# Two transformer blocks on one core: a block inversion that starts from blocks of 16, and a planner that offers other work more often

## The chip, the cores and the metric

The kernel runs on one core of a Trainium2 chip. The metric is the device time of one execution in microseconds; the number given for a kernel is the median of its runs. The profile is one further execution, recorded by the hardware profiler. Its engines are called PE (TensorE's matrix products; PEld is its loading of weights), DVE (VectorE), ACT (ScalarE), POOL (GpSimd) and SP (SyncE, which here only issues DMAs).

## What is computed

The reference chains two networks on a sequence of 512 tokens of width 1024. The first has two layers (windowed attention, neighbourhood attention, memory attention, feed-forward parts). The second is one layer with two branches beside each other, an RWKV-7 time mix and a convolution, and then a feed-forward part. The change is in the two branches:

```python
def step(S, inp):                       # RWKV-7, per head, token by token
    r_t, w_t, k_t, v_t, a_t, b_t = inp
    sa = jnp.einsum('bhvk,bhk->bhv', S, a_t)
    S = S * w_t[:, :, None, :] + sa[..., None] * b_t[:, :, None, :] + v_t[..., None] * k_t[:, :, None, :]
    y = jnp.einsum('bhvk,bhk->bhv', S, r_t)
...
c = u * jax.nn.sigmoid(gate)            # convolution branch: 31 taps per channel, then layer norm and silu
c = lax.conv_general_dilated(c, dw...) + dw_b
c = jax.nn.silu(layer_norm(c, ln_w, ln_b))
```

There are 16 heads of width 64. The kernel doesn't step through tokens: it cuts the 512 tokens into 8 chunks of 64, and within a chunk it has to invert, for each head, a 64x64 triangular matrix with ones on its diagonal.

## The kernel before, in words

**Where the change lies.** The change touches the mixing stage of the second block, some 700 us of the execution, which `drive` (line 1768) emits. Its large products are the input projections, the gates and the two output maps: units of 24 products of 128x128 by 128x512 in three passes (high by high, high by low, low by high), done by `dense` (line 1064). The units stand in a fixed list (lines 1684 to 1689): c0 to c7 are the convolution's two inputs, i0 to i7 the inputs of a pair of heads, g0 to g15 the gates, w0 to w7 the map of the RWKV branch, m0 to m7 the map of the convolution branch. A unit's weights are loaded by SP two units ahead into two buffers ("raw"), split by ACT into a high part (wh) and, in turns by DVE and by POOL, into a low part (wl).

**The streams.** Beside the units run seven generators, the streams: `outs` prepare a pair of heads (`pair_out`, with the gram matrices X and RA), `solves` invert the triangular matrices of a group of two pairs (`solve`, line 1314), `chains` carry the state S through the 8 chunks of a group (`chain`, line 1439), `posts` normalise and gate its result (`post`, line 1480), `mapped_rows` prepare the map's operand, and `ends` does the layer norm of the convolution branch. There are four groups, g = 0 to 3, and for each a solve, a chain and a post, in that order. w0 and w1 do a part of their products and then hold until the fourth post is done; the m units wait for the layer norm.

**How the order is set.** PE's and DVE's instructions stand in the order in which the program emits them. That order is set by a planner (class `Clock`, line 88), which estimates each instruction's cost (`cost`, line 122) and keeps a time for each engine. `dense` yields after each second product of its first two passes, and after some of its last. At each yield `burst` (line 1771) steps those streams whose results the planner takes to be ready: at a full burst all of them, at a minor one only those that last yielded neither BURST nor FREE, so mostly those that have no products next. Line 1078 makes every yield whose count is a multiple of 8 full and the others minor; a unit's last yield is full too.

**The taps.** The convolution's 31 taps for 8 blocks of channels (`conv`, line 1525; acc is the sum) are 240 DVE instructions, dealt out by the class `Taps` (line 199). `until(t)` emits taps while the planner's DVE time plus 0.75 is at most t. It is called after each burst with PE's planned time less 1 us (lines 1792 and 1812), and by the planner ahead of every other DVE instruction, up to the time when that one's operands are ready.

**The solve.** The diagonal 32x32 blocks of each triangular matrix are inverted first. Before the change: the 8x8 diagonal blocks travel through DRAM into the tile x, in a layout with one small matrix per partition, twice 64 partitions; DVE inverts them by seven steps of a product and a sum (lines 1364 to 1367); they travel back and are read as 32x32 blocks (dd), which DVE transposes (dt). Then two doublings follow on PE, 8 to 16 and 16 to 32. Each is made of three `quad`s: 64 products of 32x32 on four tiles of PE beside each other (the trace counts each as two, in two passes), the first of a doubling with the identity added by one product of 512 columns. ACT copies each result out. The first doubling takes the tile e as its operand, which ACT fills from the matrices with a mask. After that come the step from 32 to 64 and the application to the other operands.

Of the kernel before, what the change touches and what calls it, by code (L numbers as in the profile page):

```python
# [16 lines left out]
AF = mybir.ActivationFunctionType  # L17
ALU = mybir.AluOpType
# [4 lines left out]
P = 128  # L23
# [64 lines left out]
class Clock:  # L88
# [33 lines left out]
    def cost(self, engine, op, out, ins):  # L122
        n = max(math.prod(x.shape[1:]) for x in [out, *ins])
        if op == "dma_start":
            n, wide = math.prod(out.shape), len(out.shape) > 2 and out.shape[-1] < P
            return 0.65 if engine == "POOL" else 0.4 if not wide else 0.8 if n == 8192 else 0.65
        if engine == "DVE":
            return (0.21 if op == "scalar_tensor_tensor" else 0.14) + n * (0.00215 if op.endswith("scan") else 0.00107)
        if engine == "ACT":
            return 0.17 + n * 0.00086  # L130
        if op == "memset":
            return 0.1 + n * 0.0008
        return 2.0 if n == 8 else 0.35 + n * 0.0019
# [83 lines left out]
def tile_two_blocks(ctx: ExitStack, tc: tile.TileContext, A, out):  # L217
# [782 lines left out]
    with ExitStack() as es:  # L1000
# [63 lines left out]
        def dense(hl, xh=lambda k: hT_h[:, k, :], xl=lambda k: hT_l[:, k, :], ks=range(KD), ps=None):  # L1064

            h, l = hl
            ps = pst() if ps is None else ps
            n = 0
            for part in range(2):
                for k in ks:  # L1070
                    if part:
                        nc.tensor.matmul(ps, lhsT=l[:, k, :], rhs=xh(k), start=False, stop=k == KD - 1)
                    else:
                        nc.tensor.matmul(ps, lhsT=h[:, k, :], rhs=xh(k), start=k == 0, stop=False)
                        nc.tensor.matmul(ps, lhsT=h[:, k, :], rhs=xl(k), start=False, stop=False)
                    n += 2 - part
                    if n % 2 == 0 and (n < 3 * len(ks) or len(ks) < KD):
                        yield n % 8 != 0
            return ps


# [232 lines left out]
        def solve(g, G):  # L1314
# [4 lines left out]
            def q32(i):  # L1319
                return slice(32 * i, 32 * i + 32)  # L1320

            def d8(t, r):

                return bass.AP(t.tensor, t.offset + 264 * r, [[1024, 64], [32, 8], [1, 8]])

            def quad(lhsT, rhs, eye=False):

                ps = pst("po")
                if eye:
                    nc.tensor.matmul(ps, lhsT=ident, rhs=i32[:, None, :].to_broadcast([P, 16, 32]), start=True, stop=False)  # L1330
                for c in range(16):
                    for i in range(4):
                        nc.tensor.matmul(ps[q32(i), q32(c)], lhsT=lhsT(i)[:, c, :], rhs=rhs(i)[:, c, :],
                                         start=not eye, stop=c == 15 or not eye, tile_position=(32 * i, 32 * i))
                return ps.rearrange("p (q t) -> p q t", t=32)

            def s2(n):
                return el.tile([P, 16, 32], F32, tag="s2", name=n, bufs=3)

            def of(t):  # L1340
                return lambda i: t[q32(i)]
# [1 line left out]
            diag = [ABf[q32(i), :, q32(i % 2)] for i in range(4)]  # L1343

            x = s2("x").rearrange("p q t -> p (q t)")
            at, tt = (x[:, 128 * i : 128 * i + 128].rearrange("p (m a b) -> p m a b", m=2, a=8) for i in range(2))
            pr = x[:, 256:]
            nc.gpsimd.memset(tt, 0.0)
            nc.gpsimd.memset(tt.rearrange("p m a b -> p m (a b)")[:, :, ::9], 1.0)
            yield from there(ab)  # L1350
            for r in range(4):
                nc.sync.dma_start(at[64 * (r // 2) : 64 * (r // 2) + 64, r % 2], d8(ab, r))

            e = s2("e")
            nc.gpsimd.memset(e, 0.0)
            for i in range(4):
                for m in range(2):
                    cols = slice(16 * m + 8, 16 * m + 16)
                    nc.scalar.activation(e[q32(i), :, cols], diag[i][:, :, cols], AF.Copy,
                                         scale=blk[q32(i), P + 33 + m : P + 34 + m])  # L1360
                nc.gpsimd.memset(diag[i][:, :, 0:16], 0.0)
                nc.scalar.activation(diag[i][:, :, 16:], diag[i][:, :, 16:], AF.Copy, scale=blk[q32(i), P : P + 1])
            yield from there(at)
            for t in range(1, 8):
                p4 = pr[:, : 2 * t * t].rearrange("p (m j s) -> p m j s", m=2, s=t)
                nc.vector.tensor_tensor(p4, tt[:, :, :t, :t], at[:, :, None, :t, t].to_broadcast([P, 2, t, t]), ALU.mult)
                nc.vector.tensor_reduce(tt[:, :, :t, t], p4, AX.X, ALU.add)
            yield from there(tt)
            for r in range(4):
                nc.sync.dma_start(d8(td, r), tt[64 * (r // 2) : 64 * (r // 2) + 64, r % 2])  # L1370
            yield from there(td)
            dd, dt = s2("dd"), s2("dt")
            for i in range(4):
# [2 lines left out]
            nc.vector.transpose(dt, dd)  # L1376
            yield BURST

            de = s2("de")
            nc.scalar.activation(de, quad(of(e), of(dt), True), AF.Copy)  # L1380
            yield BURST
            dd_, dt = s2("dd"), s2("dt")
            nc.scalar.activation(dt, quad(of(dd), of(de)), AF.Copy)
            yield FREE
            nc.scalar.activation(dd_, quad(of(de), of(dd)), AF.Copy)
            dd = dd_
            yield BURST
            de = s2("de")
            nc.scalar.activation(de, quad(lambda i: diag[i], of(dt), True), AF.Copy)
            yield BURST  # L1390
# [377 lines left out]
        def drive():  # L1768
# [20 lines left out]
            def stand():  # L1789
                t = clock.free("PE")  # L1790
                clock.t["PE"] = min([s[1] for s in streams if s[1] > t] + [t + 0.5])
                taps.until(clock.t["PE"] - 1)
                burst()

            raws = [u[0]() for u in units[:2]]
# [1 line left out]
            for i, (_, _, run, pre, *_) in enumerate(units):  # L1797
                t = clock.free("PE")
                while pre is not None and not pre():
                    stand()  # L1800
                idle += clock.free("PE") - t
                if i + 2 < len(units):
                    raws.append(units[i + 2][0]())
                nxt, more = None, i + 1 < len(units)
                for n, at_ in enumerate(run(hl) if run is not None else ()):
                    if at_ == HOLD:
                        while posts_done < 4:
                            stand()
                    if more and (at_ == SPLIT or (n == 3 and not units[i][4:])):
                        nxt, more = units[i + 1][1](raws.pop(0)), False  # L1810
                    burst(at_ is True)
                    taps.until(clock.free("PE") - 1)
                if more:
                    nxt = units[i + 1][1](raws.pop(0))
                hl = nxt
# [52 lines left out]
```

## Time and profile before

| | |
|---|---|
| median of 3 runs | 2426.93 us (2425.42 to 2431.42) |
| the profiled execution | 2429.3 us, span 2427.5 us from its first to its last instruction |
| mean granted TensorE clock | 0.969 of full speed |
| PE busy | 2313.3 us, 95% of the span |
| DVE busy | 1198.5 us, 49% |
| ACT busy | 965.3 us, 40% |
| POOL busy | 339.0 us, 14% |

How to read it: 1.8 us of the execution lie outside the span. Busy times of PE overlap a little, because products are pipelined. A low granted clock makes the same product take longer. Line numbers of most rows are those of two helpers (L152 and L192 for what the planner places, L186 for the rest), so rows are told apart by their tiles.

### The profile page before, as it was taken

The numbers are of one execution on the slowest core, as the hardware profiler recorded it, in microseconds if no ns is written. First come the engines' busy times: TensorE is split into PE (matmuls) and PEld (weight loads), VectorE is DVE, ScalarE is ACT, GpSimd is POOL, SyncE is SP. The second block draws the span as 40 slices with busy tenths as digits, with TensorE's granted clock in tenths as the row PEclk, the third lists the DMA queues.
The fourth block names the chain that finished last, engine by engine and source line by source line (L and its number), as shares of the span: only waits on it lengthen the run. The fifth ranks groups of instructions, "written<-read, shape, count | busy, mean of one in ns | idle before, by whom it ended". The sixth has DMA issues, their size and how long they took to land. (4 is left out here: it accounts for less than half of the span.)

```text
span 2427.5 us, 38347 instructions
## 1 busy us (share of the span) xinstructions
PE 2313.3 (95%) x15723; PEld 1862.5 (77%) x15723; DVE 1198.5 (49%) x1832; ACT 965.3 (40%) x1743; POOL 339.0 (14%) x457
## 2 busy tenths in 40 slices
PE   7899999999999999999999889999998699999998
PEld 6756788888798788888887677777776577888886
DVE  4366533234523653223355767778786655422232
ACT  4355423123434543222334645456633523322221
POOL 1000120000200000000012332354333221000000
PEclk9889999999999999999999899999999799999999
DMA  7330673224453144333232232234244254433331
GB/s 205 100 88 18 173 223 109 78 86 131 130 148 105 61 129 123 99 96 96 87 98 88 82 82 76 62 110 112 76 114 156 83 156 165 139 96 96 97 100 55
DMA packets 326543, 262.60 MB, mean 108 GB/s; under 512 B 47152, under 2 KB 294004, under 8 KB 325984
## 3 DMA queue, kind: packets, MB, share of 16 engines
q1 hardware_dynamic: 308552, 211.18, 29.9%
q10 hardware_dynamic: 9080, 22.37, 3.2%
q0 software_dynamic: 8736, 26.61, 3.1%
q8 instruction: 123, 2.02, 0.3%
q14 instruction: 52, 0.43, 0.1%
HBM read 225.81 MB, written 34.31 MB: 107 GB/s over the span
## 5 line engine op out<-in xcount | busy, mean ns | idle before, releaser
L186 PE MATMUL p<-hT_h,wh 128*128 128x512 f32 (+1 forms) x1376 | 511.8, 377 | 7.9 <-ACT qT L186 5.8
L186 DVE TENSOR_TENSOR wl<-raw,wh 128x1024 fp32r<-128x1024 f32 (+1 forms) x270 | 319.6, 1187 | 400.0 <-ACT wh L186 352.6
L186 PE MATMUL p<-hT_l,wh 128*128 128x512 f32 (+1 forms) x1376 | 511.4, 376 | 0.0
L186 ACT ACTIVATE wh<-raw 128x1024 fp32r<-128x1024 f32 (+1 forms) x270 | 275.8, 1025 | 547.6 <-PE p L186 370.6
L186 PE MATMUL p<-hT_h,wl 128*128 128x512 f32 (+1 forms) x1376 | 327.2, 375 | 0.0
L186 PEld LDWEIGHTS p<-hT_h,wh 128*128 128x128 f32 x1376 | 260.8, 190 | 56.3 <-ACT qT L186 6.2
L186 PEld LDWEIGHTS p<-hT_l,wh 128*128 128x128 f32 x1376 | 261.0, 190 | 46.9 <-issue 0.6
L186 PEld LDWEIGHTS p<-hT_h,wl 128*128 128x128 f32 x1376 | 247.5, 189 | 46.5 <-DVE wl L186 0.2
L186 POOL TENSOR_SCALAR rstd<-ss 128x1 f32<-128x1 f32 x52 | 18.6, 358 | 1467.0 <-ACT junk L186 1466.8
L152 DVE SCALAR_TENSOR_TENSOR acc<-c,dwc,acc 128x512 f32<-128x512 f32 x240 | 209.8, 877 | 6.7
L186 PE MATMUL p<-wh,fh 128*128 128x512 f32 x528 | 205.7, 390 | 0.7 <-DVE prm L186 0.7
L186 PE MATMUL p<-wl,fh 128*128 128x512 f32 x528 | 205.8, 390 | 0.0
L186 PE MATMUL p<-wh,fl 128*128 128x512 f32 x528 | 205.2, 389 | 0.0
L192 PE MATMUL p<-hT_h,wh 128*128 128x512 f32 x448 | 188.8, 421 | 2.9 <-ACT ls L152 2.1
L192 PE MATMUL p<-hT_l,wh 128*128 128x512 f32 x448 | 180.7, 403 | 0.6 <-issue 0.6
L186 DVE TENSOR_TENSOR fT<-sg,p 128x384 f32<-128x384 f32 (+1 forms) x88 | 46.8, 552 | 254.3 <-PE p L186 247.5
L192 PE MATMUL p<-hT_h,wl 128*128 128x512 f32 x448 | 120.6, 413 | 2.6 <-DVE wl L152 2.6
L152 ACT ACTIVATE wh<-raw 128x1024 fp32r<-128x1024 f32 (+1 forms) x78 | 77.4, 992 | 114.2 <-PE p L192 57.3
L186 DVE TENSOR_TENSOR fl<-fT,fh 128x512 fp32r<-128x512 f32 x66 | 45.1, 691 | 145.4 <-ACT fh L186 145.4
L186 PEld LDWEIGHTS p<-wh,fh 128*128 128x128 f32 x528 | 99.1, 188 | 21.5 <-ACT fh L186 0.9
L186 PEld LDWEIGHTS p<-wh,fl 128*128 128x128 f32 x528 | 99.1, 188 | 20.4
L186 PEld LDWEIGHTS p<-wl,fh 128*128 128x128 f32 x528 | 99.1, 188 | 20.3
(304 smaller groups left out, 3546.1 us busy)
## 6 DMA issues: line engine op xcount, KB each, us to landing
raw<-in_w_gu SPq DMA_DIRECT2D x88, 512.0 KB
raw<-in_w_in SPq DMA_DIRECT2D x56, 512.0 KB
raw<-in_w_down SPq DMA_DIRECT2D x44, 512.0 KB
raw<-in_ffn_w_gate SPq DMA_DIRECT2D x22, 512.0 KB
raw<-in_ffn_w_up SPq DMA_DIRECT2D x22, 512.0 KB
raw<-in_ffn_w_down SPq DMA_DIRECT2D x22, 512.0 KB
raw<-in_w_in_b SPq DMA_DIRECT2D x20, 512.0 KB
xs<-xt POOLq DMA_DIRECT2D x19, 512.0 KB, 4.2
```

The source lines that it names most:

```text
L152: return f(*a, **k)
L186: return f(*a, **k)
L192: return f(*a, **k)
```

## The change

Four edits. In `solve`, the inversion on DVE starts from 16x16 diagonal blocks, in fifteen steps, one matrix per partition on 128 partitions; the doubling from 8 to 16 with its three quads and the tile e falls away; the copies of x go by two DMAs in place of four each way. In `dense`, a full burst comes at every count that is a multiple of 4. Taps are emitted up to 1.5 us past PE's planned time, where it was 1 us short of it. The planner counts 0.05 us more for each scalar_tensor_tensor on DVE.

```diff
-            return (0.21 if op == "scalar_tensor_tensor" else 0.14) + n * (0.00215 if op.endswith("scan") else 0.00107)
+            return (0.26 if op == "scalar_tensor_tensor" else 0.14) + n * (0.00215 if op.endswith("scan") else 0.00107)
...
-                        yield n % 8 != 0
+                        yield n % 4 != 0
...
-                return bass.AP(t.tensor, t.offset + 264 * r, [[1024, 64], [32, 8], [1, 8]])
+                return bass.AP(t.tensor, t.offset + 528 * r, [[1024, 64], [32, 16], [1, 16]])
...
-            nc.gpsimd.memset(tt, 0.0)
-            nc.gpsimd.memset(tt.rearrange("p m a b -> p m (a b)")[:, :, ::9], 1.0)
+            at, tt = (x[:, 256 * i : 256 * i + 256].rearrange("p (a b) -> p a b", a=16) for i in range(2))
+            pr = s2("pr").rearrange("p q t -> p (q t)")
+            nc.gpsimd.memset(x[:, 256:], 0.0)
+            nc.gpsimd.memset(x[:, 256::17], 1.0)
             yield from there(ab)
-            for r in range(4):
-                nc.sync.dma_start(at[64 * (r // 2) : 64 * (r // 2) + 64, r % 2], d8(ab, r))
-
-            e = s2("e")
-            nc.gpsimd.memset(e, 0.0)
+            for r in range(2):
+                nc.sync.dma_start(at[64 * r : 64 * r + 64], d16(ab, r))
+
             for i in range(4):
-                for m in range(2):
-                    cols = slice(16 * m + 8, 16 * m + 16)
-                    nc.scalar.activation(e[q32(i), :, cols], diag[i][:, :, cols], AF.Copy,
-                                         scale=blk[q32(i), P + 33 + m : P + 34 + m])
...
-            for t in range(1, 8):
-                p4 = pr[:, : 2 * t * t].rearrange("p (m j s) -> p m j s", m=2, s=t)
-                nc.vector.tensor_tensor(p4, tt[:, :, :t, :t], at[:, :, None, :t, t].to_broadcast([P, 2, t, t]), ALU.mult)
-                nc.vector.tensor_reduce(tt[:, :, :t, t], p4, AX.X, ALU.add)
+            for t in range(1, 16):
+                p3 = pr[:, : t * t].rearrange("p (j s) -> p j s", s=t)
+                nc.vector.tensor_tensor(p3, tt[:, :t, :t], at[:, None, :t, t].to_broadcast([P, t, t]), ALU.mult)
+                nc.vector.tensor_reduce(tt[:, :t, t], p3, AX.X, ALU.add)
             yield from there(tt)
-            for r in range(4):
-                nc.sync.dma_start(d8(td, r), tt[64 * (r // 2) : 64 * (r // 2) + 64, r % 2])
+            for r in range(2):
+                nc.sync.dma_start(d16(td, r), tt[64 * r : 64 * r + 64])
...
-            de = s2("de")
-            nc.scalar.activation(de, quad(of(e), of(dt), True), AF.Copy)
-            yield BURST
-            dd_, dt = s2("dd"), s2("dt")
-            nc.scalar.activation(dt, quad(of(dd), of(de)), AF.Copy)
-            yield FREE
-            nc.scalar.activation(dd_, quad(of(de), of(dd)), AF.Copy)
-            dd = dd_
-            yield BURST
...
-                taps.until(clock.t["PE"] - 1)
+                taps.until(clock.t["PE"] + 1.5)
...
-                    taps.until(clock.free("PE") - 1)
+                    taps.until(clock.free("PE") + 1.5)
```

## Rows read from the trace of the kernel before

**Rows 1.** Busy time of each engine by stretch; PEclk is the granted clock
```profile
1285.00:1885.00 600.00, 561.24 (x7192) 437.31 (x7191) 445.49 (x665) 323.25 (x621) 220.14 (x259) 0.96 0.34 97
1857.00:1921.00 64.00, 37.41 (x241) 26.73 (x240) 42.06 (x72) 28.32 (x48) 13.92 (x13) 0.71 0.20 60
```
**Rows 2.** Waits of PE from 1850 to 1925 us: total, times, longest
```profile
PE p L192 <- DVE ssum L152: 12.3, 1, 12.3
PE p L192 <- DVE SV L152: 6.1, 4, 4.0
PE p L192 <- DVE BKT L152: 5.4, 1, 5.4
PE p L192 <- ACT X L152: 1.7, 1, 1.7
PE p L192 <- ACT asum L152: 1.0, 1, 1.0
```
**Rows 3.** Timeline of PE, tail of the mixing stage: start, us, instruction, idle before
```profile
1878.24 0.45 PE L192 MATMUL p<-SV,X 128*64 128x64 f32 x8
...
1879.80 0.45 PE L192 MATMUL p<-SV,BKT 128*64 128x64 f32 x8 [0.88 <-DVE SV L152]
...
1881.32 0.45 PE L192 MATMUL p<-SV,X 128*64 128x64 f32 x8 [0.69 <-DVE SV L152]
...
1916.08 0.63 PE L192 MATMUL p<-X,wh 128*128 128x512 f32 x1
...
1921.06 0.40 PE L192 MATMUL p<-X,wh 128*128 128x512 f32 x1
```
**Rows 4.** Timeline of PE in the first and the last group's solve
```profile
1424.85 1.03 PE L192 MATMUL p<-blk,ident 128*128 128x512 f32 x2
1425.81 1.29 PE L192 MATMUL p<-dt,e 32*32 32x32 f32 x128
1427.03 0.50 PE L192 MATMUL p<-hT_h,wh 128*128 128x512 f32 x1
...
1435.12 1.46 PE L192 MATMUL p<-de,dd 32*32 32x32 f32 x128
...
1780.30 1.15 PE L192 MATMUL p<-blk,ident 128*128 128x512 f32 x2
...
1790.23 1.29 PE L192 MATMUL p<-dd,de 32*32 32x32 f32 x128
...
1794.26 1.15 PE L192 MATMUL p<-blk,ident 128*128 128x512 f32 x2
```
**Rows 5.** Timeline of PE around one burst of the last chain
```profile
1841.67 0.40 PE L192 MATMUL p<-hT_l,wh 128*128 128x512 f32 x1
1842.00 0.45 PE L192 MATMUL p<-SV,X 128*64 128x64 f32 x8
...
1844.66 0.45 PE L192 MATMUL p<-SV,BKT 128*64 128x64 f32 x8
...
1845.42 0.50 PE L192 MATMUL p<-hT_h,wh 128*128 128x512 f32 x1
1845.76 0.40 PE L192 MATMUL p<-hT_l,wh 128*128 128x512 f32 x1
1845.99 0.40 PE L192 MATMUL p<-hT_h,wh 128*128 128x512 f32 x1
...
1847.47 0.45 PE L192 MATMUL p<-SV,X 128*64 128x64 f32 x8
```
**Rows 6.** Timeline of DVE in the first and the last group's small inversion
```profile
1394.32 2.83 DVE L152 TENSOR_TENSOR x<-x 128x18 f32<-128x18 f32 x1
...
1764.65 0.16 DVE L152 TENSOR_TENSOR x<-x 128x2 f32<-128x2 f32 x1 [1.78 <-DMA x<-abd]
1764.84 0.16 DVE L152 TENSOR_REDUCE x<-x 128x2 f32<-128x2 f32 x1
...
1767.45 0.35 DVE L152 TENSOR_TENSOR x<-x 128x98 f32<-128x98 f32 x1
1767.84 0.26 DVE L152 TENSOR_REDUCE x<-x 128x14 f32<-128x98 f32 x1
```
**Rows 7.** All instructions on the tile x: min/median/max ns
```profile
L152 DVE TENSOR_TENSOR x<-x x28: 154/237/2835, 1393.5 to 1767.5; 128x2 f32<-128x2 f32 x4, 128x8 f32<-128x8 f32 x4, 128x18 f32<-128x18 f32 x4, 128x32 f32<-128x32 f32 x4
L152 SPq DMA_DIRECT2D x<-abd x16: 604/636/1435, 1384.9 to 1761.2; - x16
```
**Rows 8.** Waits of PE (1285 to 1850 us), SP's queue and ACT (to 1890)
```profile
PE p L192 <- DVE wl L152: 2.6, 1, 2.6
...
SPq L152 <- DVE x L152: 23.6, 4, 13.0
...
ACT wh L152 <- DMA raw<-in_w_in: 9.1, 4, 3.7
```
**Rows 9.** Timeline of DVE at the end of the taps and of the layer norm
```profile
1882.63 2.32 DVE L152 SCALAR_TENSOR_TENSOR acc<-c,dwc,acc 128x512 f32<-128x512 f32 x3
...
1937.77 2.45 DVE L152 TENSOR_TENSOR ct_l<-acc,ct_h 128x512 fp32r<-128x512 f32 x1
```
**Rows 10.** The m units' first operand on PE: first and last start
```profile
L192 PEld LDWEIGHTS p<-ct_h,wh x64: 187/188/329, 1953.4 to 2000.5; 128*128 128x128 f32 x64
```

More of the change, by code (lines that the diff above doesn't have):

```diff
@@ L1320, in q32, with d16 @@
                 return slice(32 * i, 32 * i + 32)
-            def d8(t, r):
-                return bass.AP(t.tensor, t.offset + 264 * r, [[1024, 64], [32, 8], [1, 8]])
+            def d16(t, r):
+                return bass.AP(t.tensor, t.offset + 528 * r, [[1024, 64], [32, 16], [1, 16]])
             def quad(lhsT, rhs, eye=False):
@@ L1345, in solve @@
             x = s2("x").rearrange("p q t -> p (q t)")
-            at, tt = (x[:, 128 * i : 128 * i + 128].rearrange("p (m a b) -> p m a b", m=2, a=8) for i in range(2))
-            pr = x[:, 256:]
-            nc.gpsimd.memset(tt, 0.0)
-            nc.gpsimd.memset(tt.rearrange("p m a b -> p m (a b)")[:, :, ::9], 1.0)
+            at, tt = (x[:, 256 * i : 256 * i + 256].rearrange("p (a b) -> p a b", a=16) for i in range(2))
+            pr = s2("pr").rearrange("p q t -> p (q t)")
+            nc.gpsimd.memset(x[:, 256:], 0.0)
+            nc.gpsimd.memset(x[:, 256::17], 1.0)
             yield from there(ab)
-            for r in range(4):
-                nc.sync.dma_start(at[64 * (r // 2) : 64 * (r // 2) + 64, r % 2], d8(ab, r))
-            e = s2("e")
-            nc.gpsimd.memset(e, 0.0)
+            for r in range(2):
+                nc.sync.dma_start(at[64 * r : 64 * r + 64], d16(ab, r))
             for i in range(4):
-                for m in range(2):
-                    cols = slice(16 * m + 8, 16 * m + 16)
-                    nc.scalar.activation(e[q32(i), :, cols], diag[i][:, :, cols], AF.Copy,
-                                         scale=blk[q32(i), P + 33 + m : P + 34 + m])
                 nc.gpsimd.memset(diag[i][:, :, 0:16], 0.0)
```

## Prediction

> **What bounds the kernel now.** I read the busy times by stretch first, then PE's waits in the stretch where PE is idle most, then the timelines of PE and DVE there. Up to 1885 us the mixing stage is bound by PE's queue: 561.2 of 600 us busy, while DVE is busy 445.5 us [rows 1]. The reader should see there that DVE has a quarter of its time free and PE only 39 us. From 1857 to 1921 us it is otherwise: PE is busy 37.4 of 64 us, and the granted clock is 0.71, between its two levels of 1.2 and 2.4 GHz [rows 1]. There the fourth chain ends, its post follows, and the layer norm works on the same DVE. PE's waits in it, 12.3 us for the norm's sum, 6.1 us for the chain's SV, 5.4 us for the post's result and 2.7 us for two smaller ones [rows 2], make up the 26.6 us that are idle. So the stage has two limits: the amount of work on PE, and at its end the chain solve, chain, post of the last group, beside which no large products are left.
>
> **The removed doubling.** In the first group the identity and the first quad take from 1424.85 to 1427.03 us, 2.18 us, and the next quads 1.46 and 1.29 us [rows 4]. That is 4.9 us for a group, 20 us for four. All of it is on PE's queue, which is nearly full, so I count it whole: **-20 us** (bounds: 0 if PE only waits longer for the tail, -24 if each quad took 1.46 us and its two switches, below, go too). ACT loses three copies and eight fills of e for each group; POOL loses a memset; that is off the path, because ACT is busy 323 and POOL 220 of 600 us [rows 1].
> The trace shows the 128 records of a quad in 1.29 us, 10 ns each, so the four tiles do work beside each other [rows 4]. By the Trainium skill (TensorEngine Tiling (Array Packing), Instruction Overhead) a matrix product has some 60 cycles of overhead, however few its columns, which at 2.4 GHz would make a quad 128 x 25 ns = 3.2 us if its products followed one another. By that page the removed part would be worth 4 x (1.0 + 3 x 3.2) = 42 us, an estimate; the trace disagrees, and the sum goes by the rows.
>
> **The larger inversion on DVE.** Before, 14 instructions run from 1764.65 to 1768.10 us, 3.45 us [rows 6]. After, there are 30, over 1240 elements a partition (the sum of t squared to 15) in place of 280. No row shows steps over 98 elements. The slope from 2 to 98 elements is 0.19 us / 96 = 2.0 ns for a product and 0.10 / 96 = 1.04 ns for a sum [rows 6], so 15 x 0.16 + 1240 x 0.0020 = 4.9 us and 15 x 0.16 + 1240 x 0.00104 = 3.7 us, and 30 gaps of 0.04 us: 9.8 us, 6.3 us more. If elements cost nothing beyond 98, it is 2 us less. Four groups: 25 us of DVE. DVE has 154 us free up to 1885 [rows 1], so this hides unless someone waits behind the block. Behind it stand the low parts of the next weights. Before, PE waited once for one, 2.6 us [rows 8], just when a product of 18 elements took 2.83 us instead of 0.2 [rows 6]. Half of the weights are split by POOL, so two of four blocks should meet DVE's turn: 2 x 3 us, **+6 us** (bounds 0 and 25, the whole growth).
> That one product took 2.83 us, while the median of all 28 is 237 ns [rows 6, 7]. By the Trainium skill (SBUF — State Buffer, SBUF: two separate sides) VectorE with two SBUF inputs and GpSimd exclude each other for a whole instruction. By that page each of the 60 products may be held up so, and if 8 more of them met a hold-up of 2.6 us DVE would grow by another 21 us, an estimate, and the slow rival below would lose 36 us in place of 15; in the rows it was rare, and the sum leaves it out.
>
> **SP.** Two DMAs stand for four each way, with as many pieces in all, each twice as long. An issue took 636 ns [rows 7]; one of twice the pieces is bounded by 636 and 1272 ns, so SP gains between 10 us over the stage and nothing: 0, since issues with more pieces are the nearer case. But SP waited 23.6 us in four waits, at most 13.0, for the inversion [rows 8], and raw weights stand behind that wait; ACT already waited 9.1 us for them [rows 8]. Each wait grows by up to 6 us: **+2 us** (0 to 8).
>
> **Full bursts twice as often.** A burst costs PE two switches: 0.33 us from a large product to the chain's (1841.67 to 1842.00), and 0.34 us to the next large one, where 0.23 is usual [rows 5]; so 0.21 us. From 1285 to 1890 us the timeline holds 110 such bursts, 73 of them exactly 8 large products after the one before. By the code there are 56 steps with products in the outs, 48 in the solves (36 after), 64 in the chains and 12 in the posts, so 168 after the change. If all came apart, that is 58 more, 12 us; two thirds, the share now at the shortest spacing, gives **+8 us** (0 to 12).
>
> **What the finer bursts give.** A chunk of the last chain takes 5.47 us with eight large products in each half (1842.00 to 1847.47), and 3.08 us with none (1878.24 to 1881.32) [rows 3, 5]. Four products less in each half give 5.47 - 8 x 0.23 = 3.6 us, still above the bare 3.08. For the six chunks or so that have filling work this is 11 us off the last chain. The last solve loses the 14.0 us from 1780.30 to 1794.26 [rows 4], gains 6 us in its inversion, and its nine later steps save up to 0.9 us each, 8 us. So solve, chain and post end some 27 us earlier against the units, as much as PE's idle time at the end. With it would go the low clock: 0.71 over 64 us [rows 1] means 37 us at the low level; the idle time, mostly among them, leaves some 12 busy, so 6 us (a product is 0.63 us long at 1916 us and 0.40 at 1921 [rows 3]). The bounds are 0 and -33 us. I take **-24 us**: the sizes match, but the last post must still be waited for in part.
>
> **Taps ahead, and 0.05 us more for each.** These fill DVE before its next operand is there, so the taps end earlier (now at 1885 us [rows 9]) and the layer norm can move away from the post, which the term before needs. In exchange each DVE result of a chain may stand behind 1.5 us of taps more. If the taps' own lead is lost to no one, it costs nothing; if every fourth chain step, 16 of 64, waits 0.9 us on PE, +15. Nearest are the chain's few waits, 6.1 us in all [rows 2]; I take **+3 us** (-5 to +15).
>
> **Sum.** -20 + 6 + 2 + 8 - 24 + 3 = -25 us. The profiled execution took 2429.3 us (a span of 2427.5 and 1.8 around it), 2.4 above the median, so 2404.3 there and **2402 us** as a median.
>
> **Rivals.**
> - *The tail stays.* The planner places steps by its own latencies, and if chain and post end no earlier against the units, the last term is 0: 2429.3 - 1 = 2428, 2426 as a median, no change. The taps' lead may also do nothing, as the planner already fills DVE up to each operand's time. Against it: the doubling's 14 us lie on that very chain.
> - *DVE ends the tail: slower.* If DVE doesn't use its free time better, taps and layer norm move back by the inversion's 25 us and one held-up product of 2.6 us [rows 6], 28 in all. The norm's last result is written at 1937.77 + 2.45 = 1940.2 us [rows 9] and the m units start at 1953.4 us [rows 10], so 13 us cover it; the rest is lost: +15 us, 2444, 2442 as a median. PE's savings would then only make it wait. It decides once the taps end more than 13 us after 1885 us. For it: DVE gets longer blocks. Against it: the lead puts taps in its idle quarter.
> - *Everything hides.* The whole 33 us of the tail go, and blocks, SP and taps cost nothing: -20 - 33 + 8 = -45, 2382 as a median.
>
> **How the numbers follow.** A measurement of this kernel can tell about 0.3%, 7 us, from no change. Chances: forecast 0.58 (its own range 2387 to 2419), tail stays 0.13, slower by DVE 0.16, everything hides 0.13. The forecast's and the last case are faster: 0.71, a little of the first spilling into no change: 0.13; slower 0.16. The range runs from 2376 (just past the best case) to 2436, which takes in the unchanged case and the slower bounds of blocks and taps, and leaves out the full slow rival.
>
> **What would show it.** Right: no product with e, three quads fewer in each group, 30 DVE instructions on x in 9 to 11 us, large products mostly in runs of 4, the taps ending before 1870 us, the waits at the tail's end under 10 us and a clock near 1 there. Wrong: taps that end later than now, a wait of the m units for the norm, waits for DVE's low weights of several us right after each inversion, or more bursts than 168.

## The result, and the profile after

The changed kernel takes 2459.97 us in the median of 4 runs (2452.83 to 2464.52), the kernel before 2426.69 us in 4 runs of the same comparison: a ratio of 1.0127, with a 95% interval of 1.0102 to 1.0153. It is 1.3% slower, where 1% faster was forecast.

The profiled execution took 2459.7 us, with a span of 2457.9 us, 30.4 us more than before. Two times cut the span into three: T0, the first product on the tile lo, where the mixing stage starts, and the m units' first product. From the instructions on the tiles lo and ct_h of the kernel before (count, min/median/max ns, first to last start):
```profile
L192 PE MATMUL p<-lo,wh x48: 385/492/607, 1291.5 to 1673.3; 64*128 64x512 f32 x32, 128*128 128x512 f32 x16
L192 PE MATMUL p<-ct_h,wh x64: 393/393/628, 1953.6 to 2000.7; 128*128 128x512 f32 x64
```
The same rows of the changed kernel:
```profile
L192 PE MATMUL p<-lo,wh x48: 385/486/504, 1286.9 to 1666.1; 64*128 64x512 f32 x32, 128*128 128x512 f32 x16
L192 PE MATMUL p<-ct_h,wh x64: 394/394/796, 1980.0 to 2031.2; 128*128 128x512 f32 x64
```
Up to T0 the span is 4.6 us shorter, from T0 to the m units it is 693.1 us in place of 662.1, 31.0 longer, and from there to the end 477.9 in place of 473.9, 4.0 longer. So the loss lies before the m units. The timeline of PE of the changed kernel around that place (start, us, instruction, idle before and who ended it):
```profile
1948.97 2.53 PE L192 MATMUL p<-X,wl 128*128 128x512 f32 x8 [2.66 <-DVE wl L152]
1959.01 2.07 PE L192 MATMUL p<-asum,oneD 128*128 128x512 f32 x2 [7.51 <-POOL asum L152]
1971.51 1.84 PE L192 MATMUL p<-oneD,ssum 128*128 128x2 f32 x8 [10.42 <-DVE ssum L152]
1976.01 1.12 PE L192 MATMUL p<-ident,asum 128*128 128x128 f32 x4 [2.66 <-ACT asum L152]
1979.97 0.80 PE L192 MATMUL p<-ct_h,wh 128*128 128x512 f32 x1 [2.85 <-ACT ct_h L152]
```
The last product of the w units ends at 1951.5 us. Then PE has only the layer norm's few products until 1980.0, 28.5 us. Before, there was no such gap: the m units followed the w units at once. The timeline of DVE shows what the norm had to wait for; in the code, `layer_norm` goes on only when the last tap is out (line 1578):
```profile
1952.15 5.46 DVE L152 SCALAR_TENSOR_TENSOR acc<-c,dwc,acc 128x512 f32<-128x512 f32 x7
...
1961.75 1.89 DVE L152 TENSOR_TENSOR RA<-RA,asum 128x512 f32<-128x512 f32 x3 [4.13 <-ACT asum L152]
```
The last tap ends at 1957.6 us, 670.7 us after T0, where it was 1885.0 [rows 9], 593.5 after T0. From there it is 22.4 us to the first m product. The busy times by stretch (sum us, then PE, PEld, DVE, ACT, POOL with instructions, granted clock, DMA share, GB/s) say the rest:
```profile
1285.00:1885.00 600.00, 542.53 (x5583) 419.38 (x5582) 424.44 (x678) 299.55 (x574) 208.43 (x252) 0.93 0.32 93
1950.00:1970.00 20.00, 3.58 (x7) 1.17 (x5) 15.08 (x24) 7.06 (x10) 1.26 (x1) 0.51 0.21 67
1970.00:1990.00 20.00, 12.92 (x29) 7.38 (x30) 12.41 (x20) 12.78 (x19) 1.66 (x1) 0.50 0.00 0
```
In the gap PE is nearly idle and the granted clock is 0.51; it is 0.50 in the next 20 us too, the lower level (1.2 GHz), while the m units already run. Up to 1885 us, where [rows 1] had 561.24 us, PE is busy 542.53. DVE is busy 424.44 us, less than before, although it has a larger inversion: some of its taps now come after 1885 us.

PE's waits from 1285 to 1960 us (total, times, longest) have a new head:
```profile
PE p L192 <- DVE wl L152: 21.7, 6, 6.6
PE p L192 <- DVE SV L152: 8.7, 9, 4.0
PE p L192 <- POOL asum L152: 7.5, 1, 7.5
```
Before, PE waited 2.6 us for DVE's low parts [rows 8]; now it is 21.7. The last inversion in DVE's timeline shows one of the places, with the low part that stood behind it:
```profile
1762.73 0.35 DVE L152 TENSOR_TENSOR pr<-x 128x1 f32<-128x1 f32 x1
...
1768.56 2.15 DVE L152 TENSOR_TENSOR pr<-x 128x144 f32<-128x144 f32 x1
...
1772.84 0.54 DVE L152 TENSOR_TENSOR pr<-x 128x225 f32<-128x225 f32 x1
1773.42 0.39 DVE L152 TENSOR_REDUCE x<-pr 128x15 f32<-128x225 f32 x1
1773.72 1.22 DVE L152 TENSOR_TENSOR wl<-raw,wh 128x1024 fp32r<-128x1024 f32 x1
```
The block lasts 11.1 us (1762.73 to 1773.81), one held-up product included. That product, 1768.56 to 1770.71, falls on a subtraction of POOL, 1767.99 to 1770.45, in POOL's timeline:
```profile
1767.99 2.46 POOL L152 TENSOR_TENSOR wl<-raw,wh 128x1024 fp32r<-128x1024 f32 x1
```
The inversions' groups over the whole stage (count, busy us, mean ns, idle before), and the taps:
```profile
L152 DVE SCALAR_TENSOR_TENSOR acc<-c,dwc,acc 128x512 f32<-128x512 f32 x240 | 216.4, 902 | 6.5
...
L152 DVE TENSOR_TENSOR pr<-x 128x1 f32<-128x1 f32 (+14 forms) x60 | 25.0, 416 | 2.0
...
L152 DVE TENSOR_REDUCE x<-pr 128x1 f32<-128x1 f32 (+14 forms) x60 | 14.5, 241 | 2.1
```
The inversions take 39.5 us of DVE, where the same groups before had 11.2 and 5.5, 16.7: 22.8 us more.

### The profile page after: what moved, and what is told of

Read it like the earlier page. It is cut to its first block, busy times and chain, and to the rows that moved or that the text cites. A ratio compares the mean times of both kernels' runs of the same rounds, so it can differ in the third digit from the quotient of the medians.

```text
span 2457.9 us, 35226 instructions
## 1 busy us (share of the span) xinstructions
PE 2309.8 (94%) x14179; PEld 1854.2 (75%) x14179; DVE 1221.9 (50%) x1896; ACT 941.3 (38%) x1695; POOL 332.1 (14%) x453
## 5 line engine op out<-in xcount | busy, mean ns | idle before, releaser
L186 PEld LDWEIGHTS p<-hT_h,wl 128*128 128x128 f32 x1376 | 247.4, 188 | 46.5 <-DVE wl L186 0.3
L152 DVE SCALAR_TENSOR_TENSOR acc<-c,dwc,acc 128x512 f32<-128x512 f32 x240 | 216.4, 902 | 6.5
L192 PE MATMUL p<-hT_h,wl 128*128 128x512 f32 x448 | 132.7, 435 | 19.0 <-DVE wl L152 19.0
L192 PEld LDWEIGHTS p<-hT_h,wl 128*128 128x128 f32 x448 | 88.5, 206 | 41.6 <-DVE wl L152 20.9
```

Of the source, the lines that this page charges most:

```text
L152: return f(*a, **k)
L186: return f(*a, **k)
L192: return f(*a, **k)
```

## The experiments

All 18 are in this table, in the order in which they ran. The three columns of times are from each profile, counted from that kernel's own T0: the end of the last tap, the end of the w units' last product, and the first m product. T0 itself lay between 1276.0 and 1294.3 us. "Inversion" is the solve of the changed kernel put into the kernel before.

| kernel | median us | ratio to before (95%) | taps end | w end | m start |
|---|---|---|---|---|---|
| before | 2426.69 | | 594 | 662 | 662 |
| changed | 2459.97 | 1.0127 (1.0102 to 1.0153) | 671 | 665 | 693 |
| inv_alone | 2448.99 | 1.0093 (1.0069 to 1.0117) | 659 | 651 | 681 |
| all_but_inv | 2439.04 | 1.0072 (1.0047 to 1.0096) | 608 | 678 | 677 |
| changed_fewer_taps | 2399.74 | 0.9898 (0.9881 to 0.9914) | 578 | 648 | 648 |
| changed_short_inv | 2409.16 | 0.9930 (0.9911 to 0.9949) | 596 | 648 | 648 |
| bursts_alone | 2433.22 | 1.0025 (1.0007 to 1.0043) | 622 | 660 | 660 |
| taps_alone | 2442.76 | 1.0060 (1.0035 to 1.0084) | 576 | 678 | 678 |
| cost_alone | 2433.04 | 1.0016 (0.9999 to 1.0033) | 634 | 657 | 663 |
| inv_more_pool | 2429.77 | 1.0009 (0.9989 to 1.0028) | 635 | 643 | 661 |
| changed_lead_back | 2462.87 | 1.0133 (1.0099 to 1.0166) | 670 | 639 | 692 |
| inv_all_pool | 2434.59 | 1.0013 (1.0000 to 1.0027) | 619 | 679 | 678 |
| changed_all_pool | 2444.07 | 1.0060 (1.0040 to 1.0081) | 628 | 695 | 694 |
| before_all_pool | 2449.37 | 1.0079 (1.0052 to 1.0106) | 555 | 689 | 688 |
| inv_tap_cost_16 | 2427.16 | 0.9994 (0.9981 to 1.0007) | 637 | 645 | 661 |
| inv_tap_cost_11 | 2429.30 | 0.9998 (0.9987 to 1.0009) | 632 | 653 | 660 |
| inv_tap_cost_06 | 2425.87 | 0.9988 (0.9973 to 1.0003) | 604 | 662 | 662 |
| changed_tap_cost_11 | 2432.69 | 1.0010 (0.9993 to 1.0026) | 617 | 671 | 671 |
| inv_pool_cost_16 | 2427.34 | 0.9984 (0.9974 to 0.9993) | 626 | 649 | 656 |
| inv_pool_cost_11 | 2445.70 | 1.0057 (1.0040 to 1.0074) | 632 | 671 | 671 |

The ratios are to runs of the kernel before on the same chip, whose median lay between 2423.51 and 2430.9 us. Three readings in the expectations below differ from these columns: the gap ahead of the m units, from the end of the w units, is 28.5 us in the changed kernel and 30.5 in inv_alone (they say 36 and 38), and the lead alone moves the taps' end by 17 us (they say 33).

**Which part makes it slower.** The inversion alone (the solve's hunks of the diff, the rest as before), and everything but it:
```diff
-            for t in range(1, 8):
+            for t in range(1, 16):
...
```


> The kernel before with the larger inversion alone (blocks of 16, one doubling less); bursts, taps and planner cost as before. Theory R (the taps only get what the other work leaves of DVE: in the trace before they got 210 of the 585 us from 1300 to 1885, 0.36, so 25 us of new work ahead of them moves their end by 25/0.36 = 70 us, and the layer norm and the m units wait for that end): taps end at 1940 to 1960 us, a gap on PE ahead of the m units of 20 us or more, 2445 to 2470 us. Rival B (the finer bursts and the taps ahead cost the time, by switches, waits and low clock): this kernel has neither, gains the removed quads, and takes 2405 to 2425 us with taps ending before 1915.

```diff
-                        yield n % 8 != 0
+                        yield n % 4 != 0
...
-                taps.until(clock.t["PE"] - 1)
+                taps.until(clock.t["PE"] + 1.5)
...
```


> The change without the larger inversion: full bursts at every fourth product, taps up to 1.5 us ahead, 0.05 us more per scalar_tensor_tensor, inversion from blocks of 8 as before. Theory R: taps end within 20 us of 1883, no gap ahead of the m units, 2410 to 2435 us. Rival B: as slow as the changed kernel or nearly, 2440 us or more, with PE waits and low clock as there.

The inversion alone gives most of the loss, and the same picture. DVE's timeline ends its taps here, and the m units start 22.4 us after the last one, as in the changed kernel:
```profile
1929.58 5.47 DVE L152 SCALAR_TENSOR_TENSOR acc<-c,dwc,acc 128x512 f32<-128x512 f32 x7
```
The w units, in contrast, end 11 us earlier after T0 than before (651 for 662), and the m units do not get it. The busy times from T0 to the end of the w units, before and here:
```profile
1291.50:1953.79 662.29, 603.11 (x7360) 470.12 (x7360) 482.64 (x717) 354.81 (x665) 239.44 (x267) 0.94 0.34 97
1276.00:1926.88 650.88, 582.18 (x5801) 457.00 (x5800) 474.50 (x740) 315.38 (x592) 225.33 (x262) 0.93 0.33 99
```
and the head of PE's waits here:
```profile
PE p L192 <- DVE wl L152: 20.2, 4, 8.6
PE p L192 <- DVE SV L152: 14.7, 12, 4.0
```
PE is busy 20.9 us less. Some 4 us of that are the norm's products, which stood ahead of the last w products before and stand behind them here, so the removed quads are worth some 17. PE is idle 9.5 us more: 17.6 us more for low parts and 7.5 more for SV, but 12.3 us less for the norm's sum [rows 2], a wait that now comes after the w units. So a good part of the 11 us is the norm's wait moved, not time won. Everything but the inversion has no gap, as expected, but is slower by 0.7%, 4 us above theory R's range and just under rival B's: its w units end 15 us later.

**Is it the amount of DVE work?** Two kernels take work off DVE: one ends each block's taps after 24, the other stops the larger inversion after its seventh step.
```diff
-                for t in range(1, 31):
+                for t in range(1, 25):
```


> The changed kernel with 25 of the 31 taps for each block of channels; the last six taps are left out, 48 instructions of some 0.88 us, 42 us of DVE. Nothing on PE changes. Theory R: taps end before 1905 us, the gap on PE ahead of the m units (36 us in the changed kernel) is under 10 us, and the time falls by 25 to 40 us, to 2420 to 2435. Rival B, or a theory in which the blocks on DVE hurt only through the waits for low weights right behind them: the time falls by less than 10 us.

```diff
-            for t in range(1, 16):
+            for t in range(1, 8):
```


> The changed kernel with the inversion's loop stopped after seven of fifteen steps (the other eight columns of each block are left out); three quads fewer on PE, two DMAs each way, bursts, taps and planner cost as in the changed kernel. Theory R: some 24 us of DVE go, taps end before 1900 us, PE's waits for low weights fall from 21.7 us to under 8, and the time falls by 35 to 60 us, to 2400 to 2425. Rival B: only the waits behind the blocks go, 2440 us or more. Theory D (the two larger DMAs each way are late and hold the chain): 2445 us or more with the solve as long as in the changed kernel.

Both close the gap; the first gains more than expected (2399.74 us for 2420 to 2435). With 48 taps fewer, 43 us by the 902 ns of one, the taps end 93 us earlier. The instructions on ct_h show the m units' start, 1.0% faster than before in the end:
```profile
L192 PE MATMUL p<-ct_h,wh x64: 392/394/632, 1925.9 to 1972.7; 128*128 128x512 f32 x64
```
The second is the clearest check on the forecast: with the long half of the inversion away, the rest of the change is worth -0.7%, 17 us, and PE waits 5.3 us for low parts. So without the inversion's growth on DVE the change gives two thirds of the forecast's -25. Its DMAs are those of the changed kernel, so these are not what makes the change slow.

**The other edits one by one.** The finer bursts, the lead and the planned cost, each alone:
```diff
-                        yield n % 8 != 0
+                        yield n % 4 != 0
```


> The kernel before with a full burst at every fourth product, nothing else. Without the inversion the three small edits together cost 15 us, none of it in the tail. Theory S (switches: 27 more bursts than before at 0.21 us, and chain steps placed nearer to their operands, so more waits): 2430 to 2442 us, bursts over 125. Theory L (the taps ahead hold DVE's results back): within 5 us of the kernel before, 2419 to 2430.

```diff
-                taps.until(clock.t["PE"] - 1)
+                taps.until(clock.t["PE"] + 1.5)
...
-                    taps.until(clock.free("PE") - 1)
+                    taps.until(clock.free("PE") + 1.5)
```


> The kernel before with the taps up to 1.5 us past PE's planned time, nothing else. Theory S: within 5 us of the kernel before, taps ending 10 us earlier or more. Theory L: 2430 to 2442 us, with more waits of PE for DVE's SV, RA and rkv than the kernel before.

```diff
-            return (0.21 if op == "scalar_tensor_tensor" else 0.14) + n * (0.00215 if op.endswith("scan") else 0.00107)
+            return (0.26 if op == "scalar_tensor_tensor" else 0.14) + n * (0.00215 if op.endswith("scan") else 0.00107)
```


> The kernel before with 0.05 us more for each scalar_tensor_tensor in the planner, nothing else. Theories S and L: within 5 us of the kernel before. Theory R (the taps get what is left of DVE): the planner leaves out some 12 us of taps, so they end later by up to 30 us and there is a gap ahead of the m units of up to 15 us: 2430 to 2445 us.

The lead is the dear one: 0.6% slower. It ends the taps 17 us earlier and the w units 15 us later. The last chain shows a part of it. Before, its eight chunks took 45.6 us from the first to the last product of SV by X. In PE's timeline with the lead alone it is 63.7 us:
```profile
1839.23 0.45 PE L192 MATMUL p<-SV,X 128*64 128x64 f32 x8
...
1902.90 0.63 PE L192 MATMUL p<-SV,X 128*64 128x64 f32 x8 [2.30 <-DVE SV L152]
```
and with the finer bursts alone 34.5 us:
```profile
1852.54 0.45 PE L192 MATMUL p<-SV,X 128*64 128x64 f32 x8
...
1886.99 0.45 PE L192 MATMUL p<-SV,X 128*64 128x64 f32 x8
```
So the bursts shorten the chain by 11.2 us, and the lead lengthens it by 18. That taps then stand ahead of the SV for which PE waits is borne out in part: these waits rise from 7.2 to 12.1 us, those for RA and rkv, which theory L also had, do not rise. Of the 15 us up to the end of the w units 7 are idle time of PE; in the other 8 PE is busy longer with the same 7360 products (611.3 us for 603.1), at a mean granted clock of 0.93 for 0.94. The finer bursts bring no time even so, they cost 0.25%: the last chain starts 558 us after T0 in place of 544, and so ends no earlier. Their bursts are 139 for 110 in PE's timeline, 29 x 0.21 = 6 us more for PE; what else moves the chain's start was not tried apart. The planned cost is the odd one. It adds no work to DVE, and the taps end 40 us later, for 240 x 0.05 = 12 us of plan. Its effect on the time is small (its interval reaches 0.9999), as the w units hide most of the delay: the gap is 6.5 us. But it shows that it is the planner's DVE time that sets the taps' place, not the idle time of DVE in the trace.

**The lead taken back in the changed kernel.**
```diff
-                taps.until(clock.t["PE"] + 1.5)
+                taps.until(clock.t["PE"] - 1)
...
-                    taps.until(clock.free("PE") + 1.5)
+                    taps.until(clock.free("PE") - 1)
```


> The changed kernel with the taps held 1 us short of PE's planned time again; the rest as changed. Theory R with theory L (the lead brings the taps' end forward, 33 us in the run with the lead alone, but holds back the DVE results of the chains): the taps end later than in the changed kernel (1954), at 1960 to 1990 us, the gap ahead of the m units grows, the w units end earlier than 1951, and the time is 2460 to 2490 us. If the lead were simply harmful: 2440 to 2455 us.

The last chain in PE's timeline takes 32.4 us, and 47.2 (1830.68 to 1877.89) with the lead in the changed kernel:
```profile
1834.43 0.45 PE L192 MATMUL p<-SV,X 128*64 128x64 f32 x8
...
1866.85 0.45 PE L192 MATMUL p<-SV,X 128*64 128x64 f32 x8 [0.69 <-DVE SV L152]
```
The w units end 25 us earlier (639 for 665), and nothing of it reaches the time. The taps end where they did, and PE's waits show the 25 us as a longer wait in front of the norm:
```profile
PE p L192 <- POOL asum L152: 31.6, 1, 31.6
```
Both limits of the stage are seen here side by side: without the lead PE is done with the w units 52.5 us before the m units start.

**Can the taps get room?** First by work taken off DVE: POOL splits two of three weights, or all, in three kernels.
```diff
-        W["sub"] = [nc.vector, nc.gpsimd]
+        W["sub"] = [nc.vector, nc.gpsimd, nc.gpsimd]
```


> The larger inversion alone, and two of three weights' low parts on POOL in place of every second one. That takes some 13 subtractions of 1.22 us, 16 us, off DVE, and a third of the waits for DVE's low parts behind the blocks. Theory R: taps end up to 16/0.36 = 44 us earlier than with the inversion alone (1932 us), so the 38 us between the w and the m units mostly go: 2410 to 2430 us, level with the kernel before or faster. Theory P (POOL's 2.5 us subtractions come late for PE, or hold DVE's products up): 2440 us or more, with waits of PE for POOL's wl.

```diff
-        W["sub"] = [nc.vector, nc.gpsimd]
+        W["sub"] = [nc.gpsimd]
```


> The larger inversion alone, with all low parts of the weights on POOL. That takes some 40 subtractions of 1.22 us, 49 us, off DVE and puts some 100 us on POOL. Theory R: the taps end before 1890 us, no gap ahead of the m units, no waits for DVE's low parts behind the blocks, 2395 to 2412 us: faster than the kernel before. Theory P (POOL, with 2.5 us for each, comes late for PE, or its work holds DVE's two-input products up): waits of PE for POOL's wl of 15 us or more and 2420 us or more.

> The whole change with all low parts of the weights on POOL. Theory R: taps end before 1890 us and the gap of 36 us ahead of the m units goes, so some 40 us less than the changed kernel: 2405 to 2425 us, still above the inversion alone with the same edit, by the 5 to 15 us that the three small edits cost by themselves. Theory P: 2435 us or more.

> Control: the kernel before with all low parts of the weights on POOL. Theory R: in the kernel before the taps' end doesn't hold the m units (13 us to spare), so 49 us less of DVE work bring the taps' end forward by 50 us or more and the time by less than 10 us: 2415 to 2432 us. If DVE relief is worth as much here as with the larger inversion, so that the inversion had no part in it: 2405 us or less.

With two of three on POOL the inversion's loss is gone: 1.0009 for 1.0093. With all on POOL, no PE wait for a low part is left, and the gap is closed, yet the w units end 16 us later than before, and 28 later than in inv_alone, and the time (2434.59 us) misses the 2395 to 2412 expected. The whole change with this edit misses its range too (2444.07 for 2405 to 2425). The lines of inv_all_pool give one reason: its taps are longer than the 877 ns that they have before.
```profile
L152 DVE SCALAR_TENSOR_TENSOR acc<-c,dwc,acc 128x512 f32<-128x512 f32 x240 | 243.8, 1017 | 6.8
L152 POOL TENSOR_TENSOR wl<-raw,wh 128x1024 fp32r<-128x1024 f32 x67 | 165.3, 2469 | 138.0 <-PE p L192 55.6 <-ACT wh L152 40.0 <-ACT RA L152 30.0
```
PE's waits there have at their head those in which DVE is late with SV (14.7 us in inv_alone) and with RA (5.0):
```profile
PE p L192 <- DVE SV L152: 20.2, 15, 4.1
PE p L192 <- DVE RA L152: 17.2, 9, 5.1
```
The control, the same edit in the kernel before, is 0.8% slower, which was not expected, with taps of 983 ns. The taps end 39 us earlier there, the last chain takes 59.2 us for 45.6, and PE waits 23.3 us for SV, where it was 7.2: again earlier taps beside a later chain.

Then by the plan: the planner counts less for a tap, so that more of them fit.
```diff
-            return (0.21 if op == "scalar_tensor_tensor" else 0.14) + n * (0.00215 if op.endswith("scan") else 0.00107)
+            return (0.16 if op == "scalar_tensor_tensor" else 0.14) + n * (0.00215 if op.endswith("scan") else 0.00107)
```


> The larger inversion alone, with the planner's cost of a scalar_tensor_tensor at 0.16 in place of 0.21, so that it deals out more taps in the same planned time. A cost 0.05 higher moved the taps' end 38 us back. Theory R with order (the taps' end is set by the share that the planner gives them): taps end at 1895 to 1915 (1932 at 0.21), the m units start 15 to 35 us earlier, the w units end at most 5 us later, 2415 to 2438 us. Theory C (DVE's capacity): taps end after 1925, 2442 to 2455 us.

With 0.11 and with 0.06 at the same place:

> As the run at 0.16, with the cost at 0.11. Theory R with order: taps end at 1870 to 1895, the gap ahead of the m units is under 10 us; the w units' end sets the time: if the chains aren't held back, 2400 to 2415 us, faster than the kernel before; if they are, as with the lead (25 us), 2420 to 2440. Theory C: taps end after 1920, 2440 us or more.

> As the run at 0.16, with the cost at 0.06. Theory R with order: taps end before 1880, no gap ahead of the m units, and the chains' DVE results stand behind more taps than planned, so w units end 5 to 25 us later than with 0.11: 2405 to 2440 us. Theory C: 2440 us or more with a gap.

And 0.11 in the changed kernel, which had 0.26:

> The changed kernel with the planner's cost of a scalar_tensor_tensor at 0.11 in place of 0.26. Theory R with order: taps end before 1910 (1954 at 0.26), the 36 us ahead of the m units go for the most part, 2425 to 2445 us; the lead still costs up to 25 us before the end of the w units, so it stays above the inversion alone at 0.11. Theory C: 2452 us or more.

The taps end in the expected order, but each time 8 to 18 us later than expected (1923.8, 1912.9 and 1887.7 us); the three times lie in the expected ranges and cannot be told apart. From 0.21 over 0.16, 0.11 and 0.06 the taps end at 659, 637, 632 and 604 us and the gap shrinks from 30 over 15.5 and 7 to nothing. The w units, though, end at 651, 645, 653 and 662. At 0.06 they are where they are in the kernel before, and PE's waits show why:
```profile
PE p L192 <- DVE SV L152: 20.5, 17, 5.4
PE p L192 <- DVE wl L152: 15.3, 3, 6.9
PE p L192 <- DVE ssum L152: 10.4, 1, 10.4
```
SV and low parts together are what they are in inv_alone (35.8 for 34.9 us). New is the wait for the norm's sum, 10.4 us: with the earlier taps it stands ahead of the end of the w units again, as in the kernel before. All three are level with the kernel before, and the changed kernel gets back from 1.0127 to 1.0010. So the loss can be undone by the plan alone; the earlier end of the w units in inv_alone then goes with it.

**Both together**, two of three weights on POOL and 0.16, or 0.11, for a tap:
```diff
-        W["sub"] = [nc.vector, nc.gpsimd]
+        W["sub"] = [nc.vector, nc.gpsimd, nc.gpsimd]
...
```


> The larger inversion alone, two of three low parts on POOL, planner's cost of a scalar_tensor_tensor at 0.16. If DVE's load takes the gain back: taps end at 1885 to 1900, w units at 1925 to 1932 as with either edit alone, gap under 12 us, 2408 to 2420 us. If POOL gives with one hand what it takes with the other: 2422 us or more.

> As the run before with the cost at 0.11. If DVE's load takes the gain back: taps end before 1890, no gap, w units before 1935, 2405 to 2418 us. If POOL's work holds DVE up as much as it relieves it: w units after 1940, 2422 us or more.

The first missed the gain expected of it: 0.16% faster than before, less than the 0.3% that a measurement can tell. The second is slower, with a last chain of 50.3 us for 46.4 and w units 22 us later; why the two edits together lose what either alone does not is not shown. No kernel here that does the whole computation beats the kernel before by more than 0.3%.

## Why the prediction was wrong

**The step that failed: "so this hides".** The prediction counted the larger inversion's 25 us on DVE as hidden in DVE's 154 us of idle time. The 25 us were right (22.8 measured). But the taps get only what the plan leaves of DVE, and their end moved by far more than the work put ahead of them: 65 us for 22.8 in inv_alone, a factor of 2.9; 40 us for 12 with the planned cost, and 93 for 43 with the removed taps. The norm and the m units then waited for that end.

A share makes such factors plausible: 209.8 us of taps over 594 us are 0.35 of the engine, and 1/0.35 is 2.8. That argument is mine, and no run shows a fixed factor; that 2.9 comes so near to it is in part luck. By the code the plan counts more for the inversion than the trace has: each of its dependent instructions is planned to start 0.25 us after the one before it ends (line 136), so that the plan's own growth is 8.3 us for a group, 33 for four, an estimate, of which 65 us are 2.0 times. In the inv_tap_cost runs three equal steps of 12 us of plan moved the end by 22, 5 and 28 us, and in inv_pool_cost_11 a lower planned cost went with a later end (632 for 626). Nor do the effects of single edits add up: all three other edits together moved the taps 14 us.

**The slow rival had the mechanism, and neither of its sizes.** It said that DVE would end the tail by the way from taps over layer norm to the m units, and this is what the changed kernel, inv_alone and changed_lead_back show, with 22.4 us from the last tap to the m units in all three. Its delay of 28 us was 77. Its cover of 13 us, read between the norm's last result and the m units, was too small: the taps could have ended up to 68.6 - 22.4 = 46 us later (1885.0 to 1953.6 us, less the shortest way seen), since much of the norm only stood between the products of the w units. The whole 46 us are not to be had: in cost_alone, inv_tap_cost_11 and inv_pool_cost_16 the taps end 40, 38 and 33 us later than before, and the m units already start 6.5 to 7.1 us behind the w units, 28 to 30 us after the last tap. The two errors partly cancel: 77 - 46 = 31 us, where it had 15; that this is the 31.0 measured is no check of its own, as the 22.4 is read from the same trace. The test given for it, taps more than 13 us later, was crossed by bursts_alone too (28 us), with a gap of only 0.8 us; so that test was too strict as well.

**"The taps end earlier" (taps ahead, +3).** The lead does this alone (17 us), and not in the changed kernel (671 with it, 670 without). Its price was some 14 us alone (0.6%), near the upper bound of 15. The mechanism named there, PE waiting for the chain's results behind taps, shows in 5 us of more waits for SV; the rest it did not have. The 0.05 us for each tap was not priced at all, though it enters the plan like work: it delays the taps as much as 14 us of real work would at the inversion's factor.

**What the finer bursts give, -24.** The 11 us of the last chain came out almost to the digit (11.2 in bursts_alone). In the change the lead took them back: 47.2 us with it, 32.4 without (with both edits and the small inversion, all_but_inv, it is 39.4, so the price of the lead depends on what else is there). The prediction priced the two edits separately, although both act on the same SV. And the 26.6 us of idle time at the tail were not all the chain's and the post's to save. The longest wait was for the norm's sum, and in PE's order of the kernel before it stood ahead of the post's next products:
```profile
1901.81 1.87 PE L192 MATMUL p<-oneD,ssum 128*128 128x2 f32 x8 [12.29 <-DVE ssum L152]
1903.54 1.95 PE L192 MATMUL p<-ident,RA 128*128 128x128 f32 x8
```
Its end hangs on the taps.

**Low parts, +6.** The mechanism held, the size was 19: 21.7 us in place of 2.6, in six waits of up to 6.6, where two of 3 us were counted. One product of the last inversion was held up, 2.15 us where its neighbours took 0.38 and 0.45; that is one cause of the long block, and it fell on a subtraction of POOL. Raw weights also came later: ACT waits 21.4 us for them (9.1 in [rows 8]) and SP's queue 54.9 us for the inversion (23.6). How much of the 19 is theirs (the prediction's SP term, +2) the runs do not separate.

**What was right.** No product with e is left, the last block, less what its held-up product took beyond its neighbours' 0.4 us, lasts 9.3 us (9.8 predicted; the longest product and sum took 0.54 and 0.39 us), and the removed doubling has about the size forecast: some 17 us less busy time of PE in inv_alone, for the -20. Bursts were fewer than feared: PE's timeline has 127 up to the end of the w units, 110 before, so 17 x 0.21 = 4 us for the +8. One aside of the prediction is off: beyond 98 elements a step there are 367 a block, 1.1 us by its own slopes and not 2; it entered no term.

**What stays open.** T0 differs by up to 18 us between the profiles, also between kernels whose edits lie almost wholly behind it (1291.5 before, 1276.0 in inv_alone, whose profiled execution is the shortest of its four), and with it a part of each span; one profile of each kernel does not settle why, nor how far the table's columns move from one execution to the next. Whether an order of DVE's work by hand, not by the planner's clock, could keep both the earlier w units and the earlier taps was not tried.

## What to carry to other kernels

Idle time of an engine in a trace is not free if a planner hands it out: ask which work is served last there and what share it gets, and expect added work to delay it by a multiple of itself (here mostly two to three times, and not evenly). Slack at a join is at most the distance from the late input to the consumer, less the shortest way between them, which a trace in which nobody hurries does not show. Price edits together when they act on the same instruction: here a lead for filler work took back much of what finer steps gave to the work that it delays.

## What the hardware showed that was not expected

POOL's work holds DVE's up. All 36 taps over 1 us in before_all_pool, all 41 in inv_all_pool and 25 of 26 in the kernel before run at the same time as a tensor_tensor of POOL; of the shorter ones in before_all_pool it is 70 of 204. A tap takes 877 ns on average before, with 33 low parts on POOL, 983 with 64 (before_all_pool) and 1017 with 67 (inv_all_pool, for 865 in inv_alone): moving some 49 and 46 us of subtractions away from DVE cost it 25 and 37 us in longer taps. The number alone does not set it: with 42 to 44 on POOL a tap took 876, 914 and 978 ns (inv_pool_cost_11, inv_pool_cost_16, inv_more_pool). By the Trainium skill (SBUF — State Buffer, SBUF: two separate sides) VectorE with two SBUF inputs and a GpSimd instruction that reads SBUF exclude each other; the long taps and the held-up product agree with that. The inversion's own products met it less than the prediction's estimate by that section: 60 of them took 25.0 us, four times the last block's 4.7 without the hold-up are 19, so hold-ups took some 6 us, where the estimate had 21.

The gap costs twice: after 28.5 us with next to no products the m units start at a granted clock of 0.50, with products of 0.8 and 0.6 us for 0.39, which agrees with the 4.0 us by which the rest of the span is longer.
